# Low halves of the weights in a hybrid decoder trunk: two engines or VectorE alone

## The chip, the core and the metric

The kernel runs on one core of one Trainium2 chip. The engines of the core are TensorE (PE, with its weight loads shown apart as PEld), VectorE (DVE), ScalarE (ACT) and GpSimd (POOL); SyncE (SP) issues most of the transfers. The metric is the device time of one execution in microseconds, and the time before is the median of 3 runs.

## The reference

Two layers of a decoder trunk over 512 tokens of width 1024, all in float32. Each layer normalises its input, makes one wide projection for three attention mixers and their gates, adds the merged mixers back, then does cross-attention and a gated feed-forward part:

```python
for l in range(DEPTH):                                   # DEPTH = 2
    h = rmsnorm(x, norm_mix[l])
    (a_q, a_k, a_v, b_q, b_kc, ..., c_qa, c_kv, c_kr, g_br) = jnp.split(h @ w_in[l], offsets, axis=-1)
    o_a = swa_mixer(a_q, a_k, a_v, positions, swa_sinks[l])      # A: window of 128
    o_b = nsa_mixer(b_q, ...)                                    # B: three branches
    o_c = mla_mixer(c_qa, c_kv, c_kr, ...)                       # C: latent
    g = jax.nn.sigmoid(g_br).reshape(B, S, N_BRANCH, D)
    merged = g[:, :, 0] * (o_a @ w_br_a[l]) + g[:, :, 1] * (o_b @ w_br_b[l]) + g[:, :, 2] * (o_c @ w_br_c[l])
    x = x + merged @ w_out[l]
    x = x + cross_attn(rmsnorm(x, norm_xattn[l]), rmsnorm(mem, norm_mem[l]), w_xq[l], w_xkv[l], w_xo[l])
    h = rmsnorm(x, norm_ffn[l])
    gate_h, up_h = jnp.split(h @ w_gate_up[l], 2, axis=-1)
    x = x + (jax.nn.silu(gate_h) * up_h) @ w_down[l]
return rmsnorm(x, norm_final)
```

## The kernel before, in words

Activations are held transposed, features on the 128 partitions and the 512 tokens along the row. TensorE multiplies in a rounded float32 format, so every operand is kept as two tiles: a high half (the value rounded) and a low half (what the rounding left). A product is three matmuls (`mm3`, L311 to L313): high weight by high activation, high weight by low activation, low weight by high activation.

Weights come in units of 128 partitions by up to 1024 columns, in the order in which the program will use them. `load` fetches a unit into `wraw` (three buffers) on SP's queue. `halve` turns it into `wh`, a rounding copy on ScalarE (L247), and `wl`, which is `wraw` less `wh` (two buffers each). The subtraction goes through the helper `tt`, so every one of them has the line L166, on whichever engine. It is split by columns: with `vcols` of 8 in VectorE's hands the first `vcols`/8 of the columns are VectorE's and the rest GpSimd's. `vcols` is 6 for the very first units, 5 at the start of the mixers and through most of mixer A, 4 from A's end through mixers B and C, and 8 (all on VectorE) from the memory's projections to the end of the layer.

The mixers run in three stages per layer: the projections for A, then A's attention with projections woven into it, then B's and C's attention with gates and branch products woven in. An attention step on one tile of scores goes from TensorE (scores `s`) to VectorE (`p` and `st`, mask and row minimum, L587), ScalarE (exponential), VectorE and ScalarE (normalisation), TensorE (transpose `tp`, L523), ScalarE (`ph`) and VectorE (`pl`, both halves of the transposed weights), and back to TensorE (values, `av`, L646 and L655). Rotary embedding (`rotate`) puts one multiplication on GpSimd (`tmp<-tmp,sin`) and the rest on VectorE. GpSimd also adds up squares for the norms (`acc`) and adds branch products (`mg`).

Each engine works through its own queue in order. The order in these queues isn't the one in which the code is written: a scheduler sets it when the program is built, from durations that it assumes. So another length of one instruction moves others, on all engines.

Of the kernel before, what the change touches and what calls it, by code (L numbers as in the profile page):

```python
# [8 lines left out]
F32 = mybir.dt.float32  # L9
# [3 lines left out]
OP = mybir.AluOpType  # L13
# [100 lines left out]
def drain(stream):  # L114
    for _ in stream:
        pass
# [30 lines left out]
class Trunk:  # L147
    def __init__(self, ctx, tc, a, plan):
        self.plan, self.order, self.used, self.loaded, self.halved = plan, [], 0, 0, 0
        self.raw, self.ready, self.kept = {}, {}, ()  # L150
        self.tc, self.nc, self.a = tc, tc.nc, a
        self.vcols, self.lags = 6, (2, 4)
        self.ratio = (3.5, 1.8, 2.2, 1.6)
        self.sh = ctx.enter_context(tc.tile_pool(name="shared", bufs=1))
        self.ps = ctx.enter_context(tc.tile_pool(name="psum", bufs=2, space=PSUM))
        self.dr = ctx.enter_context(tc.tile_pool(name="dram", bufs=1, space=DRAM))
# [69 lines left out]
    def halve(self, last, cuts=1):  # L226
        nc = self.nc
        while self.halved <= min(last, len(self.plan) - 1):
            i = self.halved
            raw, n = self.raw.pop(i), self.plan[i][1] * 128  # L230
            if self.plan[i][0][0] in SUMS:
                self.ready[i] = self.halve_sum(raw, *self.plan[i][0])
                self.halved += 1
                continue
            if self.plan[i][0][0] == "w_gu":
                self.gate_raw = raw
            if self.plan[i][0] in self.kept:
                k = 2 * self.kept.index(self.plan[i][0])
                wh, wl = (self.ff.tile([128, 1024], F32R, name="kept", tag=KEEP[k + t][0], bufs=KEEP[k + t][1])
                          for t in range(2))  # L240
            else:
                wh = self.sh.tile([128, 1024], F32R, name="wh", tag="wh", bufs=2)
                wl = self.sh.tile([128, 1024], F32R, name="wl", tag="wl", bufs=2)
            n //= cuts
            c = self.vcols * n // 8
            for j in range(0, cuts * n, n):
                nc.scalar.copy(wh[:, j:j + n], raw[:, j:j + n])  # L247
                self.tt(wl[:, j:j + c], raw[:, j:j + c], wh[:, j:j + c].bitcast(F32), OP.subtract)
                if c < n:
                    self.tt(wl[:, j + c:j + n], raw[:, j + c:j + n], wh[:, j + c:j + n].bitcast(F32), OP.subtract,  # L250
                            nc.gpsimd)
            self.ready[i] = (wh, wl)
            self.halved += 1

# [801 lines left out]
    def layer(self, l, st, n, xsrc, last):  # L1056

        nc, tc = self.nc, self.tc
        x = st["x"]
        with ExitStack() as xstack:  # L1060
            with tc.tile_pool(name=f"mix{l}", bufs=1, reuse_waits="tile") as self.mx:
                self.mg = []
                oa, ob, oc, b = [], [], [], {}
                a = {}
                with tc.tile_pool(name=f"pp{l}", bufs=1, reuse_waits="tile") as self.pp:
                    self.pn, self.pb, self.pbufs = 4, 2, 5
                    self.kr = self.pp.tile([128, 512], F32, name="kr")
                    with tc.tile_pool(name=f"ab{l}", bufs=1, reuse_waits="tile") as self.at:
                        sq, skv, fq, fk, nkv = self.norm_begin(), self.norm_begin(), [], [], {}
                        lat = [self.latent_task(l, x, n, skv, fk, T_CKV + i) for i in range(2)]  # L1070
                        lat += [self.norm_end(skv, 256, nkv, bank=self.mm)]
                        lat += [self.latent_task(l, x, n, sq, fq, T_CQA + i) for i in range(3)]
                        self.mixers_ab(l, x, n, a, b, oa, ob, st, lat)
                    with tc.tile_pool(name=f"c{l}", bufs=1, reuse_waits="tile") as self.at:
                        lq, lkv, c = [], [], {}
                        mb = iter(self.merge_tasks(l, x, n, 1, ob))
                        self.mixer_c(l, x, n, lq, lkv, c, oc, mb, sq, skv, fq, fk, nkv)
                xp = xstack.enter_context(tc.tile_pool(name=f"x{l}", bufs=1, side="right", reuse_waits="tile"))
                xt = []
                for k in range(KT):  # L1080
                    t = xp.tile([128, 512], F32, name=f"x{k}")
                    nc.sync.dma_start(t, xsrc[:, k])
                    xt.append(t)
                mp = ExitStack()
                mpool = mp.enter_context(tc.tile_pool(name=f"mem{l}", bufs=1, side="right", reuse_waits="tile"))
                with tc.tile_pool(name=f"wo{l}", bufs=1, reuse_waits="tile") as wo:
                    self.vcols = 8
                    mem = self.memory(l, mpool)
                    ms = []

                    def done(m):
                        o = wo.tile([128, 2, 512], F32R, name="mo", tag="mo", bufs=8)
                        self.split(o[:, 0], o[:, 1], m, self.half)
                        ms.append((o[:, 0], o[:, 1]))

                    st = self.norm_begin()

                    def out_task(i):
                        ps = yield from self.proj(("w_out", l, i), ms)
                        yield STAGE  # L1100
                        self.tt(xt[i], xt[i], ps, OP.add)
                        self.norm_split(st, xt[i], i, l * G_LAYER + G_X)
                        self.norm_tile(st, xt[i])

                    mt = self.merge_tasks(l, x, n, 2, oc, done)
                    prep, kv = mem["prep"], [mem["kv"](i) for i in range(4)]
                    drain(skew(mt[:3] + prep[:4] + mt[3:9] + prep[4:8] + mt[9:15] + prep[8:] + kv[:1] + mt[15:]
                               + kv[1:2] + [FLUSH] + [out_task(i) for i in range(KT)] + kv[2:] + [FLUSH]))
            with tc.tile_pool(name=f"xa{l}", bufs=1, reuse_waits="tile") as xa:
                st, n = self.cross(l, st, xt, xa, mem)  # L1110
            mp.close()
            with tc.tile_pool(name=f"ff{l}", bufs=1, reuse_waits="tile") as ff:
                return self.ffn(l, st, n, xt, ff, last)

    def mixers_ab(self, l, x, n, a, b, oa, ob, st, lat):
        w = lambda t: ("w_in", l, t)
        self.vcols = 5
        drain(skew([self.norm_end(st, D, n), self.k_task(w(T_AK), x, n, a, "k"), self.v_task(w(T_AV), x, n, a, "v"),
                    self.q_task(w(T_AQ), x, n, a, 0), self.compress_task(l, x, n, 0, b),
                    self.q_task(w(T_AQ + 1), x, n, a, 1)]))  # L1120
        fill = skew([self.misc_task(l, x, n, b), self.q_task(w(T_AQ + 2), x, n, a, 2),
                     self.compress_task(l, x, n, 1, b), self.q_task(w(T_AQ + 3), x, n, a, 3),
                     self.k_task(w(T_KS), x, n, b, "ks"), self.v_task(w(T_VS), x, n, b, "vs"),
                     self.q_task(w(T_BQ), x, n, b, 0, True), self.k_task(w(T_KW), x, n, b, "kw")])
        weave(self.attend(self.jobs_a(l, a, oa)), fill, self.ratio[0])
        self.vcols = 4
        ma = self.merge_tasks(l, x, n, 0, oa)
        drain(skew([self.v_task(w(T_VW), x, n, b, "vw"), ma.pop(0), FLUSH,
                    self.cmp_task(b, 0), ma[0], self.q_task(w(T_BQ + 1), x, n, b, 1, True)]))
        cmp = [self.cmp_task(b, t) for t in range(4)]  # L1130
        q = [self.q_task(w(T_BQ + t), x, n, b, t, True) for t in range(4)]
        fill = skew(ma[1:5] + [cmp[1], ma[5], q[2]] + ma[6:8] + [cmp[2]] + ma[8:10] + [q[3]] + ma[10:12]
                    + [cmp[3]] + lat[:2] + ma[12:14] + lat[2:3] + ma[14:] + lat[3:])
        weave(self.attend(self.jobs_b(b, ob)), fill, self.ratio[1])
# [459 lines left out]
```

## Time and profile before

| | us |
|---|---|
| median of 3 runs | 2041.33 (2040.67 to 2041.83) |
| the profiled execution | 2039.96 |
| its span, first to last instruction | 2038.3 |
| TensorE busy in it | 1980.4 (97%) |
| VectorE busy | 1377.7 (68%) |
| ScalarE busy | 1197.7 (59%) |
| GpSimd busy | 404.3 (20%) |

The profiled execution has 1.7 us outside its span. Layer 0 runs from the start to about 1010 us, layer 1 from there to the end; in each, the first 470 us or so are the mixers. A view by stretch tells how long each engine was busy in one stage. A timeline tells what an instruction waited for: the brackets hold the idle time before it and what ended that. A busy TensorE is not a TensorE at its peak, since the ends of its matmuls are modelled; so a small wait can be hidden in a long matmul.

### The profile page before, as it was taken

Reading aid. Unit: us, or ns where it says so; the run is one execution under the profiler, and the core shown is the slowest. Engines: PE = TensorE matmul, PEld = TensorE weight load, DVE = VectorE, ACT = ScalarE, POOL = GpSimd, SP = SyncE. Lnnn points to the kernel's source line nnn. Section 1 sums busy time; section 2 is a strip of 40 time slices with the busy share of each in tenths; the row PEclk is TensorE's granted clock in tenths of the full one; section 3 lists DMA queues with packets and bytes.
Section 4 is the critical chain, followed back from the end, with each engine's and each line's share of the span. In section 5 each row is a group of like instructions: output and inputs, shape, how many; then the busy total and the mean of one; then the engine's idle time right before and its main releaser. Section 6 shows DMA issues by size and latency. Waiting matters only on the chain. (4 is left out here: it accounts for less than half of the span.)

```text
span 2038.3 us, 31137 instructions
## 1 busy us (share of the span) xinstructions
PE 1980.4 (97%) x11368; PEld 1691.3 (83%) x11368; DVE 1377.7 (68%) x2734; ACT 1197.7 (59%) x2408; POOL 404.3 (20%) x346
## 2 busy tenths in 40 slices
PE   7999999999999999999999999999999999999998
PEld 5877887877888798989878788877788877989897
DVE  7786767666556884757567867676655578658475
ACT  4777786775446562534456767867744565435252
POOL 5332213232211300100133222223122021001000
PEclk9999999999999999999999999999999999999999
DMA  5422112224332563745343221132333334657442
GB/s 182 112 69 67 58 57 65 89 82 133 105 104 73 150 173 117 175 136 135 114 126 105 60 70 58 45 99 65 117 111 100 102 112 119 167 144 189 114 108 72
DMA packets 85745, 218.02 MB, mean 107 GB/s; under 512 B 11208, under 2 KB 17096, under 8 KB 85592
## 3 DMA queue, kind: packets, MB, share of 16 engines
q1 hardware_dynamic: 75800, 197.16, 31.6%
q0 software_dynamic: 9792, 18.88, 5.7%
q8 instruction: 89, 1.46, 0.3%
q14 instruction: 64, 0.52, 0.1%
HBM read 200.23 MB, written 4.75 MB: 101 GB/s over the span
## 5 line engine op out<-in xcount | busy, mean ns | idle before, releaser
L247 ACT CAST wh<-wraw 128x1024 fp32r<-128x1024 f32 (+3 forms) x275 | 277.4, 1009 | 374.8 <-PE mm L312 207.3
L311 PE MATMUL mm<-xh,wh 128*128 128x512 f32 x928 | 383.8, 414 | 8.6 <-ACT wh L247 6.8
L312 PE MATMUL mm<-xl,wh 128*128 128x512 f32 x928 | 373.2, 402 | 4.1 <-DVE xl L176 4.1
L313 PE MATMUL mm<-xh,wl 128*128 128x512 f32 x928 | 373.5, 403 | 2.5 <-DVE wl L166 2.3
L166 DVE TENSOR_TENSOR wl<-wraw,wh 128x1024 fp32r<-128x1024 f32 (+5 forms) x275 | 295.9, 1076 | 77.3 <-ACT wh L247 71.0
L166 POOL TENSOR_TENSOR wl<-wraw,wh 128x512 fp32r<-128x512 f32 (+4 forms) x112 | 162.6, 1453 | 513.8 <-ACT wh L247 394.9
L313 PEld LDWEIGHTS mm<-xh,wl 128*128 128x128 f32 x928 | 176.5, 190 | 43.5 <-DVE wl L166 4.7
L311 PEld LDWEIGHTS mm<-xh,wh 128*128 128x128 f32 x928 | 176.9, 191 | 42.8 <-ACT wh L247 7.2
L312 PEld LDWEIGHTS mm<-xl,wh 128*128 128x128 f32 x928 | 177.4, 191 | 40.3 <-DVE xl L176 7.0
L593 ACT ACTIVATE p<-p,st 128x256 f32<-128x256 f32 (+5 forms) x288 | 155.3, 539 | 42.8 <-DVE st L587 38.8
L173 DVE TENSOR_TENSOR pl<-tp,ph 128x256 fp32r<-128x256 f32 (+3 forms) x288 | 131.1, 457 | 49.7 <-ACT ph L172 48.4
L166 DVE TENSOR_TENSOR x<-x,mm 128x512 f32<-128x512 f32 (+1 forms) x88 | 55.6, 637 | 153.9 <-PE mm L313 153.7
L605 ACT ACTIVATE p<-p,st 128x256 f32<-128x256 f32 (+3 forms) x288 | 142.4, 532 | 28.8 <-DVE st L166 17.4
L172 ACT CAST ph<-tp 128x256 fp32r<-128x256 f32 (+3 forms) x288 | 112.9, 394 | 41.1 <-PE tp L523 38.6
L270 POOL DMA_DIRECT2D sum<-in_w_gu x36 | 43.7, 1238 | 455.8 <-DMA sum<-in_w_gu 196.2
L587 DVE CUSTOM_DVE_ANT_0 p<-s,causal 128x128 f32<-128x128 f32 (+2 forms) x224 | 106.4, 477 | 40.8 <-PE s L992 16.6
L166 POOL TENSOR_TENSOR acc<-acc,tmp 128x512 f32<-128x512 f32 (+1 forms) x55 | 74.4, 1353 | 296.8 <-ACT tmp L340 136.8
L523 PE MATMUL tp<-ident,p 128*128 128x128 f32 x656 | 122.2, 278 | 9.9 <-DVE pl L173 3.4
L312 PE MATMUL mm<-h,wh 128*128 128x512 f32 x304 | 120.2, 396 | 0.0
L311 PE MATMUL mm<-h,wh 128*128 128x512 f32 x304 | 120.2, 395 | 0.0
L313 PE MATMUL mm<-h,wl 128*128 128x512 f32 x304 | 120.2, 395 | 0.0
L523 PEld LDWEIGHTS tp<-ident,p 128*128 128x128 f32 x656 | 78.4, 141 | 31.7 <-DVE pl L173 8.6
(300 smaller groups left out, 5033.4 us busy)
## 6 DMA issues: line engine op xcount, KB each, us to landing
wraw<-in_w_in SPq DMA_DIRECT2D x91, 512.0 KB, 3.6
wraw<-in_w_gu SPq DMA_DIRECT2D x52, 512.0 KB, 3.6
sum<-in_w_gu SPq DMA_DIRECT2D x36, 512.0 KB, 4.8
sum<-in_w_gu POOLq DMA_DIRECT2D x36, 512.0 KB, 5.9
wraw<-in_w_d SPq DMA_DIRECT2D x32, 512.0 KB, 4.0
wraw<-in_w_br SPq DMA_DIRECT2D x24, 512.0 KB, 3.6
up<-in_w_gu SPq DMA_DIRECT2D x36, 256.0 KB, 3.4
wraw<-in_w_xkv SPq DMA_DIRECT2D x16, 512.0 KB, 3.6
```

Of the source, the lines that this page charges most:

```text
L166: (eng or self.nc.vector).tensor_tensor(out=out, in0=a, in1=b, op=op)
L172: nc.scalar.copy(hi, src)
L173: (eng or nc.vector).tensor_tensor(out=lo, in0=src, in1=hi.bitcast(F32), op=OP.subtract)
L247: nc.scalar.copy(wh[:, j:j + n], raw[:, j:j + n])
L270: nc.gpsimd.dma_start(s, ends, accum_op=OP.add)
L311: nc.tensor.matmul(ps, wh[:, c], xh, start=i == 0, stop=False)
L312: nc.tensor.matmul(ps, wh[:, c], xl, start=False, stop=False)
L313: nc.tensor.matmul(ps, wl[:, c], xh, start=False, stop=i == len(blocks) - 1)
L523: self.nc.tensor.transpose(tp[:, j], src[:, j * 128:j * 128 + 128], self.ident)
L587: o.nc.vector.tensor_tensor_reduce(out=p, in0=self.ps.pop(i), in1=self.mask(self.blocks[i]), scale=-self.scale, scalar=self.init, op0=OP.a ...
L593: self.o.nc.scalar.activation(p, p, AF.Exp, scale=-1.0, bias=st[:, 0, i:i + 1], accum_out=st[:, 1, i:i + 1])
L605: nc.scalar.activation(self.p[j], self.p[j], AF.Copy, scale=self.st[:, 2, j:j + 1])
```

## The change

`vcols` is removed with all its settings, and `halve` makes each low half by one subtraction on VectorE over all columns of the unit. GpSimd keeps its other work. The feed-forward part, the cross-attention and the output projection had `vcols` of 8 and are built as before.

```diff
-        self.vcols, self.lags = 6, (2, 4)
+        self.lags = (2, 4)
...
             n //= cuts
-            c = self.vcols * n // 8
             for j in range(0, cuts * n, n):
                 nc.scalar.copy(wh[:, j:j + n], raw[:, j:j + n])
-                self.tt(wl[:, j:j + c], raw[:, j:j + c], wh[:, j:j + c].bitcast(F32), OP.subtract)
-                if c < n:
-                    self.tt(wl[:, j + c:j + n], raw[:, j + c:j + n], wh[:, j + c:j + n].bitcast(F32), OP.subtract,
-                            nc.gpsimd)
+                self.tt(wl[:, j:j + n], raw[:, j:j + n], wh[:, j:j + n].bitcast(F32), OP.subtract)
...
-                    self.vcols = 8
                     mem = self.memory(l, mpool)
...
         w = lambda t: ("w_in", l, t)
-        self.vcols = 5
         drain(skew([self.norm_end(st, D, n), ...
...
         weave(self.attend(self.jobs_a(l, a, oa)), fill, self.ratio[0])
-        self.vcols = 4
         ma = self.merge_tasks(l, x, n, 0, oa)
```

The built programs differ in order too. Below, the line numbers of the changed program are 4 to 7 lower than those of the one before (L311 is now L307, L442 is L438, L587 is L583, L721 is L717). The names are those of the section on the kernel; `ident,sd` is the identity times the inverse root of the first norm, whose product with ones spreads it over the partitions, and `rope` are the steps of the rotary angles.

VectorE in the first 35 us of the program, around the operation that the first norm waits for, before:

```order
L166 TENSOR_TENSOR wl<-wraw,wh 128x640
L442 SCALAR_TENSOR_TENSOR rope_188<-rope_189,rope_188 128x512
L369 RECIPROCAL sd<-sd 128x4
L166 TENSOR_TENSOR wl<-wraw,wh 128x640
L442 SCALAR_TENSOR_TENSOR rope_188<-rope_189,rope_188 128x512
L166 TENSOR_TENSOR tmp<-ident,sd 128x512
L442 SCALAR_TENSOR_TENSOR rope_188<-rope_189,rope_188 128x512
```

and now:

```order
L166 TENSOR_TENSOR wl<-wraw,wh 128x1024
L438 SCALAR_TENSOR_TENSOR rope_186<-rope_187,rope_186 128x512
L365 RECIPROCAL sd<-sd 128x4
L166 TENSOR_TENSOR wl<-wraw,wh 128x1024
L438 SCALAR_TENSOR_TENSOR rope_186<-rope_187,rope_186 128x512
L166 TENSOR_TENSOR tmp<-ident,sd 128x512
L438 SCALAR_TENSOR_TENSOR rope_186<-rope_187,rope_186 128x512 x2
```

The two subtractions are whole units now, and of the `rope` steps that stood ahead of this piece one more has gone behind `tmp<-ident,sd`.

VectorE where the first queries `q` of mixer A become ready, for which TensorE waits with its first scores, before:

```order
L166 TENSOR_TENSOR tmp<-mm,rstd 128x512
L166 TENSOR_TENSOR tmp<-tmp 128x512
L781 MEMSET kb 128x64
L166 TENSOR_TENSOR wl<-wraw,wh 128x640
L166 TENSOR_TENSOR q<-tmp,q 64x512 x2
L791 CAST vb<-causal 128x256
L587 ISA p,st<-s,window,nsink 128x128
```

and now:

```order
L166 TENSOR_TENSOR tmp<-tmp 128x512
L166 TENSOR_TENSOR v<-tp,v 128x4x64
L166 TENSOR_TENSOR tmp<-mm,rstd 128x512
L166 TENSOR_TENSOR q<-tmp,q 64x512 x2
L166 TENSOR_TENSOR wl<-wraw,wh 128x1024
L583 ISA p,st<-s,window,nsink 128x128
```

The low half of the weights stood before the queries and stands behind them now; an evacuation (`tmp<-mm,rstd`) and the last part of `v` stand between the rotary sum and the queries instead.

TensorE at the same place (`xh` and `xl` are the halves of the activations, numbered from one program to the other two lower), before:

```order
L311 MATMUL mm<-xh_149,wh 128x512
L312 MATMUL mm<-xl_150,wh 128x512
L721 MATMUL s<-k,q 128x128
L722 MATMUL s<-k,q 128x128
L721 MATMUL s<-k,q 128x256
```

and now:

```order
L307 MATMUL mm<-xh_147,wh 128x512
L308 MATMUL mm<-xl_148,wh 128x512
L309 MATMUL mm<-xh_147,wl 128x512
L307 MATMUL mm<-xh_151,wh 128x512
L308 MATMUL mm<-xl_152,wh 128x512
L309 MATMUL mm<-xh_151,wl 128x512
L307 MATMUL mm<-xh_155,wh 128x512
L717 MATMUL s<-k,q 128x128
```

Five weight products that stood behind the first scores stand ahead of them.

VectorE in mixer B of layer 0, about 163 us into the program before, where TensorE waits for `pl`, before:

```order
L166 TENSOR_TENSOR of<-av,tmp 64x256
L166 TENSOR_TENSOR wl<-wraw,wh 128x512
L173 TENSOR_TENSOR pl<-tp,ph 128x4x128
L587 ISA p,st<-s,causal 128x128
L587 ISA st 128x1
L601 RECIPROCAL st<-st 128x2
L166 TENSOR_TENSOR st<-st,gate 128x2
```

and now:

```order
L166 TENSOR_TENSOR of<-av,tmp 64x256
L173 TENSOR_TENSOR pl<-tp,ph 128x4x128
L597 RECIPROCAL st<-st 128x2
L166 TENSOR_TENSOR st<-st,gate 128x2
L583 ISA p,st<-s,causal 128x128
L583 ISA st 128x1
L166 TENSOR_TENSOR wl<-wraw,wh 128x1024
```

The subtraction has gone from just before `pl` to behind the next `p`.

## Rows read from the trace of the kernel before

**Rows 1.** The page: busy time of the engines, and the group of low-weight matmuls.

```profile
PE 1980.4 (97%) x11368; PEld 1691.3 (83%) x11368; DVE 1377.7 (68%) x2734; ACT 1197.7 (59%) x2408; POOL 404.3 (20%) x346
...
L313 PE MATMUL mm<-xh,wl 128*128 128x512 f32 x928 | 373.5, 403 | 2.5 <-DVE wl L166 2.3
```

**Rows 2.** Busy us by stretch: PE, PEld, DVE, ACT, POOL; clock; DMA share, GB/s.

```profile
0.00:55.00 55.00, 42.15 (x164) 30.65 (x165) 42.14 (x71) 28.35 (x44) 27.32 (x29) 1.00 0.63 184
...
105.00:150.00 45.00, 41.24 (x245) 32.50 (x243) 40.56 (x100) 34.77 (x87) 14.42 (x17) 1.00 0.21 61
150.00:335.00 185.00, 181.43 (x1010) 152.42 (x1011) 130.31 (x379) 139.74 (x331) 38.22 (x26) 1.00 0.20 61
335.00:470.00 135.00, 129.77 (x676) 105.03 (x675) 91.85 (x204) 102.82 (x229) 36.83 (x27) 1.00 0.31 93
```

**Rows 3.** Groups by form: count, busy us, mean ns of one, idle before.

```profile
L166 DVE TENSOR_TENSOR wl<-wraw,wh 128x512 fp32r<-128x512 f32 x66 | 58.3, 884 | 17.1 <-ACT wh L247 17.0
...
L173 DVE TENSOR_TENSOR S24l<-sum,S24h 128x1024 fp32r<-128x1024 f32 x36 | 44.1, 1224 | 15.8 <-ACT S24h L172 15.8
...
L166 DVE TENSOR_TENSOR wl<-wraw,wh 128x640 fp32r<-128x640 f32 x26 | 25.3, 972 | 6.6 <-ACT wh L247 4.5 <-issue 2.0
...
L173 DVE TENSOR_TENSOR q<-tmp,q 96x512 fp32r<-96x512 f32 x16 | 12.5, 820 | 10.6 <-ACT q L172 10.6
```

**Rows 4.** The same view of POOL alone: its share of the half units.

```profile
L166 POOL TENSOR_TENSOR wl<-wraw,wh 128x512 fp32r<-128x512 f32 x66 | 107.2, 1624 | 374.4 <-ACT wh L247 319.5 <-PE tp L523 28.3 <-DVE st L587 16.2
```

**Rows 5.** Timeline of DVE, attention of A and B: start, duration, instruction, idle before.

```profile
117.98 1.43 DVE L166 TENSOR_TENSOR tmp<-tmp 128x512 f32<-128x512 f32 x1
...
164.12 0.69 DVE L166 TENSOR_TENSOR wl<-wraw,wh 128x512 fp32r<-128x512 f32 x1 [0.54 <-ACT wh L247]
164.73 0.69 DVE L173 TENSOR_TENSOR pl<-tp,ph 128x512 fp32r<-128x512 f32 x1
```

**Rows 6.** Timeline of POOL in the attention of A.

```profile
117.59 1.28 POOL L166 TENSOR_TENSOR wl<-wraw,wh 128x512 fp32r<-128x512 f32 x1 [0.74 <-ACT wh L247]
```

**Rows 7.** Timeline of DVE, first 55 us.

```profile
14.92 2.29 DVE L166 TENSOR_TENSOR acc<-acc,tmp 128x512 f32<-128x512 f32 x2
...
28.63 1.49 DVE L166 TENSOR_TENSOR tmp<-ident,sd 128x512 f32<-128x512 f32 x1
...
48.76 1.47 DVE L166 TENSOR_TENSOR tmp<-tmp 128x512 f32<-128x512 f32 x1 [0.27 <-POOL tmp L166]
...
50.23 0.75 DVE L166 TENSOR_TENSOR wl<-wraw,wh 128x640 fp32r<-128x640 f32 x1
```

**Rows 8.** Timeline of POOL, the same 55 us.

```profile
14.41 1.45 POOL L166 TENSOR_TENSOR wl<-wraw,wh 128x384 fp32r<-128x384 f32 x1
...
26.48 3.10 POOL L166 TENSOR_TENSOR wl<-wraw,wh 128x384 fp32r<-128x384 f32 x2
...
48.69 0.99 POOL L166 TENSOR_TENSOR wl<-wraw,wh 128x384 fp32r<-128x384 f32 x1
```

**Rows 9.** Timeline of PE, the same 55 us: its waits behind these.

```profile
17.99 0.50 PE L313 MATMUL mm<-xh,wl 128*128 128x512 f32 x1 [0.79 <-DVE wl L166]
...
30.27 1.10 PE L375 MATMUL av<-tmp,ones 128*128 128x512 f32 x2 [0.84 <-DVE tmp L166]
...
51.75 0.33 PE L721 MATMUL s<-k,q 128*128 128x128 f32 x1 [2.62 <-DVE q L166]
```

**Rows 10.** Instructions with tile `wl` alone, busy us: PE, PEld, DVE, POOL.

```profile
105.00:150.00 45.00, 14.23 (x35) 6.57 (x35) 2.98 (x4) 7.60 (x5) 1.00 0.21 61
```

**Rows 11.** Timeline of PE at the two places of rows 5.

```profile
119.90 0.41 PE L523 MATMUL tp<-ident,p 128*128 128x128 f32 x2 [0.59 <-DVE v L166]
...
165.48 0.39 PE L655 MATMUL av<-pl,v 128*128 128x256 f32 x1 [0.34 <-DVE pl L173]
```

**Rows 12.** Busy us in two stretches of mixer B, columns as in rows 2.

```profile
170.00:180.00 10.00, 10.00 (x59) 8.63 (x58) 6.23 (x23) 6.53 (x17) 2.04 (x2) 1.00 0.19 54
...
200.00:210.00 10.00, 9.33 (x56) 7.95 (x55) 9.07 (x32) 8.00 (x20) 1.30 (x1) 1.00 0.08 14
```

## The prediction

> **What bounds the kernel now.** I read the page first, then busy time by stretch, the groups of the low halves, and the timelines where TensorE waits. TensorE is busy 1980.4 of 2038.3 us, and of all its waits before low-weight matmuls only 2.3 us are for `wl` [rows 1]. So the low halves are made early enough, and GpSimd's time on them is worth nothing by itself: the change can matter only by what it does to VectorE's queue, and there only where TensorE waits. The stretches show that this differs by stage [rows 2]. In the first 55 us TensorE idles 55 - 42.15 = 12.9 us. In the second half of A's attention VectorE is busy 40.56 of 45 us (90%) and TensorE idles 3.8. In mixer B VectorE is busy 70% and TensorE idles 3.6 of 185 us; in C 68% and 5.2 of 135. The rest of a layer, some 540 us, is not touched. All that could be gained, with nothing ever late in the mixers, is some tens of us; what matters is what VectorE does just before the few waits.
>
> **What VectorE gets.** A half unit costs VectorE 884 ns for 512 columns, and 972 ns for 640 [rows 3]; GpSimd's part of 512 columns takes 1624 ns beside it [rows 4]. The unit as one subtraction of 1024 columns isn't in the mixers of this trace; the nearest row is the same operation on the same sizes in the feed-forward part, 1224 ns [rows 3]. So the units cost 66 x (1224 - 884) + 26 x (1224 - 972) = 22.4 + 6.6 = 29 us more, and the few smaller units, by an estimate from these, some 3 more: 32 us over both layers. The 66 lie at the end of A and in B and C, 33 in each layer, so with the small ones 12.7 us a layer there.
>
> Why 884, when a subtraction of 512 columns takes 0.69 us where it is not held up [rows 5]? Because VectorE and GpSimd hold each other up. `tmp<-tmp`, two SBUF inputs, begins at 117.98 while GpSimd has been on its part of a unit since 117.59, and takes 1.43 us [rows 5, 6]; GpSimd is done at 118.87, and the other 0.54 us later. At 28.63 and 48.76 the same: 1.49 and 1.47 us beside GpSimd's subtractions from 26.48 and 48.69 [rows 7, 8]. So other operations of VectorE get time back as well. In the group of `q` of C a mean of 820 stands against 690, so 2 us in 16 of them [rows 3]; some of that is owed to work that GpSimd keeps. Over all groups I estimate 10 us back, between 0 and 18, so VectorE's load grows by some 22 us, 14 to 32, on 1378.
>
> The Trainium skill says of the ports, in "SBUF — State Buffer", section "Who interferes with whom": a VectorE instruction with two SBUF inputs and a GpSimd instruction that reads SBUF share a read interface, and the one that starts first keeps it for its whole length. The rows above agree. By that rule alone the two parts of a unit run one behind the other, GpSimd's 1.28 us [rows 6] behind VectorE's 0.69, and the whole unit on VectorE is ready earlier, not later; since TensorE waits 2.3 us for low halves in all, that is worth 2 us at most.
>
> **The start of layer 0: a gain.** Three waits of TensorE hang on VectorE there [rows 9].
> - At 17.99 it waits 0.79 us for `wl`. The two `acc` before it took 2.29 us beside GpSimd's subtraction at 14.41 [rows 7, 8]; at 0.69 each they take 1.4, so 0.9 us come back, and the unit costs 0.5 more (1.22 against 0.75 [rows 3, 7]). Gain 0.4.
> - At 30.27 it waits 0.84 us for `tmp<-ident,sd`. That was held up by 0.8 us beside GpSimd's 3.10 us from 26.48 [rows 7, 8]; one `rope` step, 0.7 at this width, has gone behind it, as the order shows; two longer units cost 1.0. The `rope` step between them was beside GpSimd too. So it comes 0.5 us sooner or more. Gain 0.7.
> - At 51.75 it waits 2.62 us for `q`. `tmp<-tmp` gets back 0.8, and the unit of 0.75 us that stood between now stands behind `q` [rows 7]; an evacuation and a part of `v`, some 1.1 us, have gone ahead, so `q` comes 0.5 us sooner. And TensorE has five weight products to do first. Gain 1.4.
>
> Sum 2.5 us, between 0 (given back in A, where VectorE is nearly full) and 4.2 (0.79 + 0.84 + 2.62). For the start of layer 1, where the projections follow the feed-forward part without such waits, I take nothing.
>
> **A's attention.** From 105 to 150 us VectorE has four half units at 2.98 us, 0.74 each [rows 10]; each becomes 1.22, 0.48 more, so 1.9 us where 90% are already taken. Against that stands the held-up `tmp<-tmp` at 117.98, behind which TensorE waits 0.59 us at 119.90 [rows 5, 11]; that wait should go. What is late next are the score banks, since `p` waits in VectorE's queue behind the longer subtraction, and with it the next scores. I take a loss of 0.5 us in each layer, between a gain of 1 and a loss of 1.9.
>
> **B and C.** 12.7 less A's 4 x 0.34 is 11.3 us a layer more for VectorE. Behind each unit stand `pl`, `p` and `of` of the attention. What hides it is VectorE's idle time, 30%: the unit at 164.12 began after 0.54 us of it. But the `pl` behind it is what TensorE waits for at 165.48, 0.34 us [rows 5, 11]. Left in that place the longer unit would make this 0.9. The scheduler has moved it behind the next `p`, as the last piece of the order shows, so this wait should end. For the price of a busier VectorE I compare two stretches of B [rows 12]: at 6.23 of 10 us busy TensorE idles 0, at 9.07 it idles 0.67, so 0.67 / 2.84 = 0.24 us per us at most, and nothing at the lower end. B and C run at 70%, near the lower end, so I take 0.07: 0.8 us a layer, between 0 and 11.3 x 0.24 = 2.7.
>
> **Sum.** -2.5 + 2 x 0.5 + 2 x 0.8 = +0.1 us on the profiled execution's 2039.96 (span 2038.3 and 1.7 outside it), so 2040.1. That execution was 1.4 us below the median of the runs, 2041.33; against the median I forecast **2041.4 us**. A measurement of this kernel can tell about 0.2% from no change, 4.1 us.
>
> **Rivals.**
> - *The collisions were the cost (faster).* All three waits at the start go (4.2), 1 us in each A, and nothing is lost in B and C: -6.2, so 2035.1. For it speak the 0.5 to 0.8 us that a collision costs VectorE. Against it: the places with collisions and those where TensorE waits coincide only a few times in a layer, and GpSimd's rotary products, `acc` and `mg` stay and meet longer subtractions.
> - *VectorE's queue becomes the bound in the attention (slower).* A unit of 1.22 us stands whole ahead of `p` and `pl`, where half a unit let them through half a us sooner. It costs 1.9 us in each A and 2.7 in each B and C, and the start keeps only 1: 2 x 4.6 - 1 = +8.2, so 2049.5. It decides where TensorE loses more than about 0.2 us for each us that VectorE gets. For it: 90% in A. Against it: 70% in B and C, and an order laid anew around the longer operation. The Trainium skill stands on this side, in "Perfetto Trace Analysis", section "Optimizing Scalar/DVE Operations": a saturated VectorE can be a reason to give work away, to GpSimd too, and where it isn't full but makes others wait, smaller instructions can help; it adds that these two share a port, so that it might not. No run here shows yet which of these holds.
> - *The subtraction doesn't come at 1224 ns in the mixers.* If 0.1 us per unit is lost to GpSimd's remaining work, half of what the 512 columns lose now (884 against 690), VectorE gets 9 us more over both layers, by 0.07 to 0.24 that is 1 to 2 us: inside the range.
>
> **How the numbers follow.** Within 0.2%: 0.52, with the third case in it. Faster by more: 0.22, the first rival and gains at the start without the losses. Slower by more: 0.26, the second rival, wholly or halfway. The range goes from 2035.5, by the first rival's end, to 2049, by the second's; it leaves out about one in ten on either side.
>
> **What would show it.** Right: VectorE busy for 1390 to 1410 us, GpSimd near 240; no `tmp<-tmp` or `tmp<-ident,sd` of 1.4 us at the start; the waits at 18 and 30 us gone, that before the first scores under 1.5 us; TensorE idle from 105 to 150 us within 1 us of 3.8, in B and C within 1.5 of 3.6 and 5.2. Wrong: several waits of TensorE in each stage for `pl` or `st` right behind a `wl` of 1.2 us (the second rival), or an attention of A that begins 3 us earlier and stays so (the first). Since the order in all queues is new, waits can come and go at places that this reading didn't look at; a few us either way would not surprise me.

## The result, and the profile after

The changed kernel takes **2028.99 us** (median of 4 runs, 2028.77 to 2030.70), against 2041.00 for the kernel before beside it: ratio 0.9946, 95% interval 0.9934 to 0.9957. It is 12 us faster; I had forecast 2041.4, and the range ended at 2035.5. The profiled execution took 2028.90 us with a span of 2027.2, so 11.1 less than before.

The page of the changed kernel, the lines that answer to [rows 1]:

```profile
PE 1977.0 (98%) x11368; PEld 1689.5 (83%) x11368; DVE 1392.9 (69%) x2734; ACT 1196.9 (59%) x2408; POOL 243.2 (12%) x234
...
L309 PE MATMUL mm<-xh,wl 128*128 128x512 f32 x928 | 371.7, 401 | 4.1 <-DVE wl L166 4.1
```

VectorE has 15.2 us more to do, GpSimd 161 less, and TensorE waits for low halves a little longer (4.1 us). So the 11 us didn't come from low halves that are ready sooner. Stretches of the changed kernel that answer to [rows 2], with ends moved to where the same work stands now (PE, PEld, DVE, ACT, POOL; clock; DMA):

```profile
0.00:53.00 53.00, 42.15 (x170) 31.26 (x171) 41.52 (x68) 26.93 (x39) 13.61 (x21) 1.00 0.63 187
103.00:147.50 44.50, 42.21 (x253) 34.03 (x252) 41.85 (x106) 36.39 (x93) 7.71 (x12) 1.00 0.24 70
147.50:330.00 182.50, 180.62 (x1007) 151.50 (x1006) 134.22 (x374) 139.02 (x327) 8.97 (x6) 1.00 0.20 60
330.00:463.50 133.50, 129.23 (x673) 104.66 (x672) 93.50 (x204) 102.46 (x230) 10.75 (x8) 1.00 0.31 94
```

TensorE's idle time goes from 12.9 to 10.9 us at the start, from 3.8 to 2.3 in the second half of A's attention, from 3.6 to 1.9 in B, from 5.2 to 4.3 in C. Groups of VectorE by form, answering to [rows 3]:

```profile
L166 DVE TENSOR_TENSOR wl<-wraw,wh 128x1024 fp32r<-128x1024 f32 x247 | 313.9, 1271 | 63.5 <-ACT wh L246 62.1
...
L166 DVE TENSOR_TENSOR tmp<-tmp 128x512 f32<-128x512 f32 x22 | 15.1, 688 | 8.5 <-POOL tmp L166 8.1
```

155 of the 247 were there before, at 1263 ns; the 92 new ones come to 118 us, 1284 each. (That takes the 155 as unchanged; the 103 whole units that stand in the mixers now have a mean of 1305.) `tmp<-tmp` is no longer held up: its mean was 793 ns before. At the start, VectorE (answering to [rows 7]) and then TensorE (to [rows 9]):

```profile
16.07 1.22 DVE L166 TENSOR_TENSOR wl<-wraw,wh 128x1024 fp32r<-128x1024 f32 x1
...
28.19 0.68 DVE L166 TENSOR_TENSOR tmp<-ident,sd 128x512 f32<-128x512 f32 x1
...
47.29 0.68 DVE L166 TENSOR_TENSOR tmp<-tmp 128x512 f32<-128x512 f32 x1
...
48.94 1.40 DVE L166 TENSOR_TENSOR q<-tmp,q 64x512 fp32r<-64x512 f32 x2
50.37 1.23 DVE L166 TENSOR_TENSOR wl<-wraw,wh 128x1024 fp32r<-128x1024 f32 x1
```

```profile
17.35 0.50 PE L309 MATMUL mm<-xh,wl 128*128 128x512 f32 x1 [1.10 <-DVE wl L166]
...
29.10 1.02 PE L371 MATMUL av<-tmp,ones 128*128 128x512 f32 x2
...
49.67 0.33 PE L717 MATMUL s<-k,q 128*128 128x128 f32 x1 [1.55 <-DVE q L166]
```

The operations of 1.49 and 1.47 us take 0.68 now. The wait at 30 us is gone, that before the first scores is 1.07 us shorter, and that at 18 us is 0.3 longer.

In B TensorE's order differs at many places. A wait that only changes its name is no gain, though. Before, TensorE around 195 us of layer 0:

```profile
195.12 0.28 PE L655 MATMUL av<-ph,v 128*128 128x256 f32 x1
195.88 0.39 PE L655 MATMUL av<-pl,v 128*128 128x256 f32 x1 [0.48 <-DVE pl L173]
```

and the same two matmuls in the changed kernel:

```profile
190.93 0.39 PE L651 MATMUL av<-ph,v 128*128 128x256 f32 x1 [0.40 <-ACT ph L172]
191.16 0.39 PE L307 MATMUL mm<-oh,wh 128*128 128x512 f32 x1
191.39 0.40 PE L308 MATMUL mm<-oh,wh 128*128 128x512 f32 x1
191.62 0.39 PE L309 MATMUL mm<-oh,wl 128*128 128x512 f32 x1
191.85 0.35 PE L651 MATMUL av<-pl,v 128*128 128x256 f32 x1
```

Three weight products stand between them now, and cover what VectorE still needs for `pl`. But a wait of 0.40 us for `ph` has come ahead of them, and from the transposes before to the last of these value products the place takes 2.0 us as it did, the three products not counted. What did get shorter is the place of [rows 5] and [rows 11]; VectorE and then TensorE there now:

```profile
159.88 0.69 DVE L173 TENSOR_TENSOR pl<-tp,ph 128x512 fp32r<-128x512 f32 x1 [0.60 <-ACT ph L172]
...
161.31 1.23 DVE L166 TENSOR_TENSOR wl<-wraw,wh 128x1024 fp32r<-128x1024 f32 x1 [0.27 <-ACT wh L246]
```

```profile
160.44 0.28 PE L651 MATMUL av<-ph,v 128*128 128x256 f32 x1
160.63 0.39 PE L651 MATMUL av<-pl,v 128*128 128x256 f32 x1
```

The subtraction stands behind `pl`, and the wait of 0.34 us is gone, as the prediction said. From the one value product to the next it is 0.19 us, where it was 0.73.

For all that follows I add up TensorE's loss by stage: how far the distance from the start of one matmul to the next goes beyond the median for that shape, from 0.06 us on. Before it is 116.7 us, after 105.6; the difference is that of the spans. The stages are cut at the first scores of A, B and C (for B those with `k`, not the earlier ones with `kb`) and at the first output projection; the last row is the repetition of a run below. Each row is one execution. The first execution of that last program, which took 3.7 us longer in all, lost 1.1 us more at the start and 2.5 more in A of layer 0, but within 0.3 us the same in A of layer 1 and in each B and C. So a difference of 2.5 us in A of layer 0 is not firm by itself; those in B and C are.

| TensorE's loss, us | start | A, layer 0 | B | C | rest | A, layer 1 | B | C | rest | all |
|---|---|---|---|---|---|---|---|---|---|---|
| before | 10.0 | 14.4 | 16.6 | 9.7 | 11.8 | 13.2 | 16.6 | 9.7 | 14.7 | 116.7 |
| after | 7.7 | 12.1 | 15.1 | 9.1 | 11.1 | 11.6 | 15.2 | 9.0 | 14.7 | 105.6 |
| whole, old order | 7.9 | 17.1 | 19.6 | 10.0 | 11.3 | 12.4 | 19.8 | 10.0 | 14.8 | 122.8 |
| split, new order | 9.0 | 13.2 | 14.6 | 9.0 | 11.4 | 12.3 | 14.9 | 9.0 | 14.4 | 107.8 |

### The profile page after: what moved, and what is told of

Its sections match the earlier page's. It is cut to its first block, busy times and chain, and to the rows that moved or that the text cites. A ratio compares the mean times of both kernels' runs of the same rounds, so it can differ in the third digit from the quotient of the medians.

```text
span 2027.2 us, 30844 instructions
## 1 busy us (share of the span) xinstructions
PE 1977.0 (98%) x11368; PEld 1689.5 (83%) x11368; DVE 1392.9 (69%) x2734; ACT 1196.9 (59%) x2408; POOL 243.2 (12%) x234
## 5 line engine op out<-in xcount | busy, mean ns | idle before, releaser
L307 PE MATMUL mm<-xh,wh 128*128 128x512 f32 x928 | 384.4, 414 | 7.8 <-ACT wh L246 6.5
L166 DVE TENSOR_TENSOR wl<-wraw,wh 128x1024 fp32r<-128x1024 f32 (+3 forms) x275 | 334.7, 1217 | 71.1 <-ACT wh L246 66.4
L307 PEld LDWEIGHTS mm<-xh,wh 128*128 128x128 f32 x928 | 176.7, 190 | 41.1 <-ACT wh L246 7.0
L583 DVE CUSTOM_DVE_ANT_0 p<-s,causal 128x128 f32<-128x128 f32 (+2 forms) x224 | 106.2, 476 | 39.6 <-PE s L859 16.1
L307 PE MATMUL mm<-h,wh 128*128 128x512 f32 x304 | 120.2, 395 | 0.0
L166 POOL TENSOR_TENSOR mg<-mg,gt 128x512 f32<-128x512 f32 x32 | 48.0, 1501 | 359.5 <-DVE gt L1040 359.3
```

The source lines that it names most:

```text
L166: (eng or self.nc.vector).tensor_tensor(out=out, in0=a, in1=b, op=op)
L307: nc.tensor.matmul(ps, wh[:, c], xh, start=i == 0, stop=False)
L583: o.nc.vector.tensor_tensor_reduce(out=p, in0=self.ps.pop(i), in1=self.mask(self.blocks[i]), scale=-self.scale, scalar=self.init, op0=OP.a ...
```

## Experiments: the work and the order apart

The change does two things: it gives VectorE whole units, and it makes the scheduler lay all queues anew. To part them I let a program be laid once with one split, note every queue's order, and build the other split in it, with edges that set only the order of issue and add no wait:

```diff
+        for k, j in zip(rank[e], rank[e][1:]):
+            tc.add_manual_dep(q[j], q[k].name, how, reason="the other program's order")
```

In the traces of the runs with a whole order, the matmuls and the instructions of VectorE and ScalarE do stand in the sequence of the program whose order was given; only GpSimd's subtractions, which one of the two programs lacks, are placed by the scheduler. Each ratio is to the kernel before on the run's own chip, where it took 2039.8 to 2040.4 us.

> The low halves are whole on VectorE, as in the changed kernel, but every queue (PE, VectorE, ScalarE, SyncE, and what GpSimd keeps) stands in exactly the order of the kernel before, forced by ordering edges without waits. Theory 'collisions' (GpSimd's subtractions held VectorE up): nearly the whole gain stays, 2029 to 2033 us, and VectorE's two-input operations take 0.69 us as in the changed kernel. Theory 'order' (the scheduler's new order made the gain): no gain or a loss, 2041 to 2047 us, since the longer subtraction stands where it stood, ahead of q and pl.

> The low halves are split between VectorE and GpSimd, as in the kernel before, but the queues of all engines stand in exactly the order of the changed kernel. 'Collisions': about as slow as the kernel before, 2038 to 2043 us. 'Order': most of the gain is there, 2029 to 2033 us. If both count, the two runs of this call lie between, and their differences to the kernel before add up to about -12 us.

> The run with the split in the new order once more, beside the changed kernel on the same chip, since its profiled execution was 2.6 us above its median: 2030 to 2034 us. What lies between it and the changed kernel, 2 to 3 us expected, is what GpSimd's parts cost in the new order.

Measured: whole units in the old order **2046.73** (ratio 1.0033, 1.0021 to 1.0045); the split in the new order **2031.74** (0.9960, 0.9947 to 0.9973) and, in the repetition, 2032.08 (0.9958, 0.9946 to 0.9971). So "collisions" falls as the main cause. With the work of before, the new order alone gains 8 us; with the order of before, the change in work alone loses 7. In the new order, taking GpSimd's parts away gains 3 us more, 0.9959 to 0.9946, which the intervals don't quite hold apart. VectorE was held up as much as ever in the run that gained 8 us (groups of the repetition):

```profile
L167 DVE TENSOR_TENSOR wl<-wraw,wh 128x512 fp32r<-128x512 f32 x66 | 61.6, 934 | 13.7 <-ACT wh L248 13.6
```

What whole units do in the old order is shown by VectorE and then TensorE at the place of [rows 5] and [rows 11]:

```profile
166.19 1.23 DVE L167 TENSOR_TENSOR wl<-wraw,wh 128x1024 fp32r<-128x1024 f32 x1 [0.53 <-ACT wh L248]
167.34 0.68 DVE L174 TENSOR_TENSOR pl<-tp,ph 128x512 fp32r<-128x512 f32 x1
```

```profile
166.82 0.38 PE L656 MATMUL av<-ph,v 128*128 128x256 f32 x1
168.07 0.39 PE L656 MATMUL av<-pl,v 128*128 128x256 f32 x1 [0.87 <-DVE pl L174]
```

The wait of 0.34 us became 0.87, as the prediction said it would "left in that place" (0.9). B loses 3 us more in each layer. With the split in the new order there is no wait at this place:

```profile
162.35 0.69 DVE L174 TENSOR_TENSOR pl<-tp,ph 128x512 fp32r<-128x512 f32 x1 [0.59 <-ACT ph L173]
...
163.78 0.69 DVE L167 TENSOR_TENSOR wl<-wraw,wh 128x512 fp32r<-128x512 f32 x1 [0.27 <-ACT wh L248]
```

```profile
162.91 0.28 PE L656 MATMUL av<-ph,v 128*128 128x256 f32 x1
163.09 0.39 PE L656 MATMUL av<-pl,v 128*128 128x256 f32 x1
```

So it is the place of the subtraction in VectorE's queue that made or ended this wait. The same shows in sum: the value products of B and C wait for `pl` 3.3 us before, 5.4 with whole units in the old order, and 0.4 in the new order with either work. Part of that comes back as waits for `ph`: 1.3 us before, 2.2 with the split in the new order, 1.4 after.

**Which queue?** Two mixtures of the orders, by engine:

> Low halves whole on VectorE; TensorE's queue in the order of the changed kernel, all other queues in the order of the kernel before. With all queues in the old order this work took 2046.7 us, with all in the new one 2029. Theory 'TensorE's order' (weight products laid ahead of scores cover the waits): most of the 17 us is got, 2030 to 2036 us. Theory 'VectorE's order' (pl, p and q laid ahead of the low half): little, 2043 to 2048 us.

> The counterpart: VectorE's and ScalarE's queues in the new order, TensorE's, SyncE's and GpSimd's in the old one; low halves whole on VectorE. 'VectorE's order': 2029 to 2035 us, and TensorE's loss in each mixer B falls from 19.7 us to 15 to 16. 'TensorE's order': 2042 to 2048 us, B stays at 19 to 20.

Measured: 2062.42 and 2046.93. Neither theory holds. TensorE's new order with the others old is the slowest kernel of all: ahead of transposes it waits 15.5 us for `pl`, against 7.6 with all queues old, and 5.3 us for `of`. VectorE's and ScalarE's new order lowers B from 19.7 to 17.0, but A of layer 0 rises from 17.1 to 23.9. So the gain belongs to the orders that were laid together; no one queue has it.

**Which stage?** Mixtures by stage:

> The split of the kernel before; the queues stand in the new order from A's end through B and C, and in the old one in what is recorded for the starts and A. Theory 'the order's gain (8.2 us with this work) lies in B and C': 2031 to 2036 us, and TensorE's loss in each B falls from 16.6 to about 14.7 us. Theory 'it lies in A': 2038 to 2041 us.

> The same mixture of orders with low halves whole on VectorE. 'The order matters in B and C': B comes down from 19.7 to about 15 us in each layer, so 10 us below the 2046.7 of the old order, 2035 to 2038 us; what is left to the changed kernel is A. 'In A': 2043 to 2047 us.

Measured: 2041.07 and 2042.54. B's loss comes down as expected, to 14.8 and 14.4 us with the split and to 15.2 and 15.2 with whole units, C's to 9.0; but A loses 18.1 and 16.4 us in the first (14.4 and 13.2 before). Work of the later stages is woven into A, and the mixture has a seam there; that this makes the loss is likely but not shown. So the profile shows the order's gain in B (2 us a layer with the split, 4.5 with whole units) and in C (0.7 to 0.9), while the total shows none of it with the split (ratio 1.0003) and, with whole units, 4 us of some 10 (2042.5 for 2046.7). These runs say nothing on A.

**Does an order suit the work for which it was laid?** Three more orders:

> Low halves whole on VectorE, all queues in a third order: the one that the scheduler lays for a program with both parts of each unit on VectorE, one behind the other. Theory 'an order laid for VectorE alone suits VectorE alone': 2028 to 2034 us. Theory 'the new order was a lucky draw': anywhere up to 2047 us, and above 2036 with even odds.

> Low halves whole on VectorE, all queues in a fourth order: the one that the scheduler lays when GpSimd has an eighth of each unit. Theory 'an order laid for nearly this work suits it': 2028 to 2034 us. Theory 'which order comes out is a draw': anywhere from 2028 to 2047 us, as the third order with 2040.

> The split of the kernel before, all queues in a fifth order: the one laid when GpSimd has a quarter of each unit everywhere in the mixers. 'An order suits the work it was laid for': 2040 us or above. 'A draw': anywhere from 2030 to 2047 us.

Measured: 2040.10, 2036.17 and 2039.10. Whole units thus took 2029.0, 2036.2, 2040.1 and 2046.7 us in four orders; the split took 2031.9, 2039.1 and 2039.9 in three. The first theory's 2028 to 2034 us fail: the third order was laid for VectorE alone too, and is no faster than the kernel before. In a weaker form it stands for whole units, which are 7 to 18 us faster in the three orders laid for whole or nearly whole units than in the one laid for the split; for the split it doesn't, since its own order is the slowest of its three. Which order comes out moves this kernel by up to 18 us with the same work, and the new one is the best of those tried for either work. Why the scheduler came to it rather than to a worse one isn't settled by these runs.

## Experiments: what GpSimd's part costs

In the new order, the split in one half of the program only:

> All queues in the new order; the units are whole on VectorE at the starts and in A, and split with GpSimd from A's end through B and C. Theory 'the held-up VectorE counts only at the starts and in A, and in B and C only the order counts': as the changed kernel, 2028 to 2030 us. Theory 'it counts everywhere': 2031 to 2033 us, near the 2031.7 of the split in the new order.

> The counterpart of the run with the split in B and C: all queues in the new order, units split with GpSimd at the starts and in A, whole on VectorE from A's end on. If the held-up VectorE counts at the starts and in A alone: as the split everywhere in the new order, 2031 to 2033 us, so 2 to 3 us above the changed kernel. If it counts nowhere by itself: 2028 to 2030 us.

Measured: 2029.82 (ratio 0.9950) and 2034.43 (0.9973, 0.9963 to 0.9983). The split in B and C costs nothing that can be told from none (0.9935 to 0.9965); at the starts and in A it costs 5 us against the changed kernel. That is more than the split everywhere costs (2031.9), but the intervals overlap. How much of it is held-up VectorE and how much GpSimd's queue, these runs don't part. The counterpart, the old settings from A's end on and whole units before, in an order of its own:

```diff
-        self.vcols, self.lags = 6, (2, 4)
+        self.vcols, self.lags = 8, (2, 4)
...
-        self.vcols = 5
+        self.vcols = 8
```

> The kernel before with one part of the change alone: units whole on VectorE at the starts and in A, split as before from A's end on, in the scheduler's own order (which in B and C is nearly that of the kernel before). If VectorE is relieved at the starts and in A as in the new order, 4 to 6 us are gained there and nothing in B and C: 2034 to 2036 us. If the order that comes out in A undoes it: 2038 to 2042 us.

Measured: 2035.71 (0.9980, 0.9971 to 0.9989), 4 to 5 us faster than before. It has an order of its own in A, so the relief of VectorE and the order aren't told apart here.

Then three kernels in the changed kernel's order, with GpSimd given back some work on each unit after VectorE's subtraction:

```diff
+                    self.tt(raw[:, j + c:j + n], raw[:, j + c:j + n], wh[:, j + c:j + n].bitcast(F32), OP.subtract, nc.gpsimd)
```

```diff
+                    nc.gpsimd.memset(raw[:, j:j + n], 0.0)
```

(In these two, half of the first unit is also still split; the third clears 8 columns.)

> The changed kernel in its own order, and after each unit GpSimd makes the subtraction that it made before once more, into the dead raw weights, where nobody waits for it. VectorE's work stays whole. 'Collisions': some 30 us of held-up VectorE come back on top of the longer subtractions, so at or above the kernel before, 2040 to 2050 us. 'Order': nothing changes, 2029 to 2031 us.

> As the run before, but GpSimd's extra instruction is a memset of the whole dead raw unit: it holds GpSimd and the raw buffer, and reads nothing. 'Collisions' by reading SBUF: no loss, 2029 to 2031 us. A rival, that GpSimd's queue (rotary products and sums of squares behind its subtractions) made the kernel before slow: 3 to 10 us of loss here, as in the run with the subtraction.

> As the run in which GpSimd clears the dead raw unit (2039.2 us), but it clears only 8 of its columns: hardly any time on GpSimd, and the raw buffer is still given back by way of GpSimd's queue. Theory 'the buffer comes back late, and SyncE's queue with the small transfers stands behind its load': 2035 to 2040 us, as with the whole clear. Theory 'GpSimd's time ahead of its other work (rotary products, sink columns)': 2029 to 2032 us.

Measured: 2050.82, 2039.15 and 2030.05. The busy time of the engines on the pages of the first two:

```profile
PE 1982.1 (97%) x11368; PEld 1692.7 (83%) x11368; DVE 1417.9 (69%) x2734; ACT 1197.9 (58%) x2408; POOL 377.4 (18%) x347
```

```profile
PE 1978.2 (97%) x11368; PEld 1690.4 (83%) x11368; DVE 1396.4 (69%) x2734; ACT 1196.9 (59%) x2408; POOL 344.4 (17%) x347
```

A GpSimd that reads makes VectorE busy for 25 us more than in the changed kernel, one that only writes for 3.5. The Trainium skill says in "SBUF — State Buffer", section "Who interferes with whom", that a two-input instruction of VectorE contends with GpSimd's reads, not with its writes; the traces agree. The reading run costs 22 us. Placed behind VectorE's own subtraction, GpSimd's reads meet other operations with two inputs in SBUF: `st<-st,gate`, on the way to the transposes, takes 325 ns in the mean for 167, and the rotary `k<-tmp,k` 845 for 706, while `p` and `pl`, which read scores or `tp` from PSUM, take what they took. B loses 20.5 us in place of 15. Not all of the 22 us are owed to the reads, since this run too holds GpSimd and the raw unit, as the writing one does.

The writing one costs 10 us all the same, so the rival named there, GpSimd's queue, is real in this order; what it cost in the kernel before isn't shown. The chain around 77 us of that run, on GpSimd, SyncE, VectorE and TensorE:

```profile
76.29 0.95 POOL L255 MEMSET wraw<- 128x1024 f32 x1
77.21 1.30 POOL L167 TENSOR_TENSOR tmp<-tmp,sin 128x512 f32<-128x512 f32 x1
```

```profile
77.28 0.34 SPq L223 DMA_DIRECT2D wraw<-in_w_in  x1
77.67 0.48 SPq L750 DMA_DIRECT2D z<-tmp  x1
```

```profile
83.71 0.58 DVE L167 TENSOR_TENSOR zp<-z,pe 128x248 f32<-128x248 f32 x1 [1.88 <-DMA z<-tmp]
...
86.36 1.22 DVE L167 TENSOR_TENSOR wl<-wraw,wh 128x1024 fp32r<-128x1024 f32 x1
87.50 0.47 DVE L591 CUSTOM_DVE_ANT_0 p<-s,window,nsink 128x256 f32<-128x256 f32 x1
```

```profile
88.03 0.39 PE L725 MATMUL s<-k,q 128*128 128x256 f32 x1 [1.45 <-DVE st L591]
```

The memset is the last user of the raw unit. Until it ends, SyncE's load of the next unit waits, and behind it the small transfer `z`; its reader `zp` stands at the head of VectorE's queue, with `q`, `wl` and `p` behind; TensorE waits for `p`'s `st`. The product `tmp<-tmp,sin` waits behind the memset too. When only 8 columns are cleared, the buffer comes back by way of GpSimd's queue just the same, and at most 1 us is lost (2030.05). So the way isn't what costs; GpSimd's time ahead of the load and of the product is.

## Experiments: further the same way

GpSimd still makes the rotary sine products. On VectorE they stand beside the rest of the rotary work:

```diff
-        self.tt(s, s, self.sin, OP.mult, self.nc.gpsimd)
+        self.tt(s, s, self.sin, OP.mult)
```

> The changed kernel in its own order, and the rotary sine products (22 of 1.44 us on GpSimd) on VectorE too, 0.7 us each; everything else stands where it stood. Theory 'a VectorE that isn't held up and doesn't wait for GpSimd gains in A': 2025 to 2029 us, since VectorE gets 15 us of work and loses 8 us of waits for GpSimd's product and some 12 us of being held up. Theory 'VectorE is full in A, and more work in its queue delays p and pl': 2030 to 2036 us.

> The same work, in the order that the scheduler lays for it. If the order suits: as the run beside it. Since it is one more draw of an order: anywhere from 2025 to 2045 us, and the difference to the run beside it is the order's alone.

Measured: 2028.14 in the changed kernel's order (0.9942, 0.9925 to 0.9958), **2022.49** in the order laid for it (0.9912, 0.9897 to 0.9927). The second is the fastest of all: 6.5 us below the changed kernel, 17.5 below the one before. The page and the group of the products:

```profile
PE 1978.2 (98%) x11368; PEld 1690.1 (84%) x11368; DVE 1399.7 (69%) x2756; ACT 1197.2 (59%) x2408; POOL 210.8 (10%) x212
...
L166 DVE TENSOR_TENSOR tmp<-tmp,sin 128x512 f32<-128x512 f32 x22 | 15.1, 685 | 1.9 <-DMA tmp<-tmp 1.8
```

VectorE gets 15.1 us of products and is busy for only 6.8 more. TensorE's loss in A goes from 12.1 and 11.6 to 8.5 and 10.0 us, elsewhere it stays within some 0.6 us. (The first scores of B come 10 us earlier in this order, so the stages don't hold quite the same work.) In the first run, with nothing moved, the work alone gains 0.9 us, which can't be told from none; the other 5.6 are the order's again.

## Why the prediction was wrong, point by point

- **What bounds the kernel: right in the main.** GpSimd's time on the low halves was worth nothing by itself. TensorE's waits that VectorE ended went from 34.8 to 25.5 us over the whole program, those that ScalarE ended only from 13.4 to 12.9.
- **What VectorE gets: right in sum, at the low end, from two terms that were both too small.** 15.2 us net, in the range of 14 to 32. Added up by instruction, the subtractions take 38.8 us more (32 forecast): the unit took 1284 ns instead of 1224 in the mixers, so the third rival came to 0.06 us a unit. All other operations take 22 us less, more than the 18 that I gave as the upper end. But `q` of C, which I had counted, still takes 820 ns.
- **The start of layer 0: right in sum, 2.3 us for 2.5 forecast.** The waits at 30 us and before the first scores shrank (the second to 1.55 us; the gain of 1.4 would have left 1.2). That at 18 us stayed: `acc` got its 0.8 us back and the low half came 0.6 us sooner (17.35 for 17.99), but TensorE was through with the products ahead of it sooner still. That the sum came so near is partly luck.
- **A's attention: the wrong sign.** 0.5 us lost in each layer was forecast, 2.3 and 1.6 were gained. The wait behind `v` at 119.90 went, as said. What was to be late next, the scores that wait for `p`'s `st`, was late at fewer places: 1.4 us at 2 places over both layers, for 3.1 at 5. The work alone, in the old order, makes it a loss of 2.7 in layer 0 and a gain of 0.8 in layer 1; the order alone gains 1.2 and 0.9. In layer 0 none of these is clearly more than what two executions of one program differ by there.
- **B and C: the wrong sign, and the failed step.** 0.8 us lost in each layer was forecast, 2.1 gained. I took the orders of before and after as alike but for single pieces, and priced the busier VectorE from two stretches of the old one that hold different work. In the old order it is dearer than my upper end: by the sum of its instructions, VectorE has 5.4 us more in B of layer 0, and TensorE loses 3.0, 0.56 us per us, not 0.07 to 0.24. In the new one whole units cost B 0.5 and 0.3 us, and the order itself gives 2.4 to 2.7 us a layer in B and C. The one wait of B that I did follow into the new order, 0.34 us, ended as said; I counted it for nothing and didn't ask how many more there are. (I also took A's four units off VectorE's load at 0.34 us each, though I had priced them at 0.48; that is 0.6 us and changes nothing.) The sum had no term for the order, though its own last sentence names it; that term is -8 us with the old work and -18 with the new.
- **The rivals.** The first, 2035.1 by collisions, was the right side with mostly the wrong cause: with the order held new, taking GpSimd's parts away gains some 3 us. The second, VectorE's queue as the bound, is real: with the order held old, whole units give 2046.7, where I had 2049.5 for it. It didn't come because the order was laid anew.
- **What would show it.** VectorE's and GpSimd's busy times came as said, and C's idle time; TensorE's idle time in A (2.3 us) and in B (1.9) fell further than the signs allowed, and A began 2.1 us earlier. I had said that other waits could come and go for "a few us either way". The same work in other orders moves by 8 to 18 us, so the range, 13.5 us wide, was built from terms that were all smaller than the one left out. How good a newly laid order is could not be read from the old trace; why this one is the best of those tried stays open.

## What to carry to other kernels

Where a scheduler lays the queues, an edit of one operation is two edits: test them apart by holding the order while the work changes, and the work while the order changes. A forecast from the old trace can hold for the old order at most; the new order needs a term and a width of its own, taken from how far the kernel moves when the same work is laid otherwise. And an order can be worth more than the work that is moved: here the work alone lost 7 us, and the new order turned that into 12 gained.

## What the runs showed of the hardware

- Operations that hold each other up need not cost time: split subtractions in B and C, with VectorE's half at 0.92 us in place of 0.69, gave 2029.8 us, within the noise of the whole ones (2029.0).
- An engine that is last to let go of a buffer sets the transfers behind it in SyncE's queue: clearing each whole raw unit on GpSimd (0.96 us) instead of 8 columns of it (0.11) cost 9 us in all (2039.15 against 2030.05), with no work added elsewhere. Part of that is GpSimd's own next work, which starts later.
- A GpSimd that writes SBUF leaves VectorE nearly alone (3.5 us more busy with 92 memsets of 0.96 us and some shorter ones), one that reads it doesn't (25 us).
